# Products of a constant on the tensor engine in a planned encoder layer, with the plan's ties drawn from names

## The chip, the cores and the metric

The kernel runs on one core of a Trainium2 chip. A core has a tensor engine (PE, whose weight loads the profile lists apart as PEld), a vector engine (DVE), a scalar engine (ACT), a general engine (POOL) and a queue engine that issues transfers (SP). Each takes its own instructions in the order in which they were written, and waits for the others by semaphores. The metric is the device time of one execution in microseconds, the median of the runs.

## The reference, cut to what matters

One encoder layer on 512 tokens of width 1024 in float32: a layer norm, a mixer that joins neighbourhood attention with a bidirectional state-space branch (SSD), a layer norm, a squared-ReLU MLP, a layer norm.

```python
def reference(x, ...):
    h = layer_norm(x, ln0_g, ln0_b)
    mix = hybrid_mixer(h, w_in, conv_w, ..., w_attn_br, w_ssd_br, b_gate, w_o)
    h = layer_norm(DN_ALPHA * h + mix, ln1_g, ln1_b)
    return layer_norm(DN_ALPHA * h + sq_relu_mlp(h, w_ff1, w_ff2), ln2_g, ln2_b)

def hybrid_mixer(u, ...):
    q, k, v, z, xbc, dt_raw, gate = jnp.split(u @ w_in, offs, axis=-1)
    ya = neighbourhood_attention(q, k, v, rpb) @ w_attn_br
    xs, bm, cm = jnp.split(silu(centred_dwconv(xbc, conv_w, conv_b)), ...)
    y = ssd forward + ssd backward + xs * d_skip
    ys = group_rms_norm(y * silu(z)) * ssd_norm_w @ w_ssd_br
    return (sigmoid(gate0) * ya + sigmoid(gate1) * ys) @ w_o
```

The change touches nothing that is computed. It acts in the first layer norm, in the first projections, and on the order of the SSD branch.

## The kernel before, in words

Every product of two matrices is written as three (`mm3`, lines 352 to 354): both operands are split into a rounded part and a remainder, and high times high, high times low and low times high are summed in PSUM. So a weight slab `ws` that was loaded becomes `wh` (a copy on ACT, line 470) and `wl` (the difference, on DVE or POOL, line 473), and the normed tokens become `hTh` and `hTl`.

**The opening.** The 512 tokens come as four tiles `xt` of 128 tokens. DVE takes mean and variance of each (lines 507, 509), a few small steps on ACT and DVE give the scale (lines 515 to 526), and DVE writes the normed tile `xn` in two halves of 512 channels (line 532). PE transposes tiles 0 and 1 (half 0 of the tokens), later tiles 2 and 3 (half 1), 128 channels at a time, into four PSUM tiles `tp_h0_0_0` to `tp_h0_0_3` of two channel blocks each (line 561). Of each channel block k = 0 to 7, ACT makes `hTh` (line 568), ACT or DVE takes the bias off again (`hmb`, lines 574 and 578; in half 0 ACT for even k, DVE for odd k), and DVE makes `hTl` (line 585). The first projections `ps_x0_0` to `ps_x0_3` (B, C and two blocks of x of SSD group 0) take half 0 of the tokens first, k by k, three products a step: tiles `ps_x0_0` and `ps_x0_1` together are 48 products over 256 tokens and read the slab `bc0`. The first product of `ps_x0_2` reads the slab `x0`. The projection of dt (`ps_dt`) follows in between.

**The order.** From here to the end of the SSD branch nothing is written in the order of its engines. Each step is handed to `Plan.op` with its engine, a guess of its time, and the tiles that it reads and writes. `Plan.order` gives every step a rank (the longest chain of guesses behind it), and walks through a guess of the run: an engine that is free takes the ready step of the highest rank, on PE a "filler" (a projection) only when no chain step is ready. PSUM tiles and buffers are granted as counted by tags (`mm` 2, `tr` 2, `cb` 1, `yd` 1, `so` 2). The steps are then issued in the order of their guessed starts, and that is final. The ranks are first multiplied by small random factors, the `NUDGES`: each pair (seed, size) draws one factor per step. Before the change the draws go by the step's place in the list.

All later stages (attention, output projection, MLP) are ordered by the framework's own scheduler, outside the plan. `ones`, a 128x128 tile of 1.0 (memset on DVE, line 411), is used by one sum in the SSD branch (line 688).

Of the kernel before, what the change touches and what calls it, by code (L numbers as in the profile page):

```python
# [3 lines left out]

# [7 lines left out]
F32 = mybir.dt.float32  # L12
# [7 lines left out]
P = 128  # L20
# [20 lines left out]
BANKS = {"mm": 2, "tr": 2, "cb": 1, "yd": 1, "so": 2}  # L41
# [19 lines left out]

NUDGES = ((265225, 0.01), (410045, 0.001), (566648, 0.0005), (745606, 0.0005), (658272, 0.001), (17203, 0.0005),
          (943025, 0.0005), (429358, 0.001), (235890, 0.0005), (366213, 0.001))
XN_ENG = (("DVE", "DVE"),) * 4
LN0_BANKS = (("tr", "tr", "yd", "so"), ("tr", "tr", "yd", "tr"))
WDT = ("DVE", 0.66)
# [4 lines left out]
class Plan:  # L73
# [4 lines left out]
    TABLE = 1.28  # L78

    def __init__(self, tags):  # L80
        self.tags, self.ops, self.tiles = tags, [], {}

    class Tile:
        def __init__(self, plan, name, tag, make):
# [16 lines left out]

    def op(self, engine, us, fn, r=(), w=(), lock=False, table=None, filler=False, at=0.0):

        self.ops.append(dict(i=len(self.ops), e=engine, us=us, fn=fn, r=list(r), w=list(w), lock=lock,
                             table=table, filler=filler, at=at))

    def order(self, nudges=()):
        ops, n = self.ops, len(self.ops)
# [4 lines left out]
        for o in ops:  # L113
            i = o["i"]
# [21 lines left out]
        for t, u in users.items():  # L136
            tag = self.tiles[t].tag
# [11 lines left out]
        rank = [0.0] * n  # L149
        topo, deg = [], [len(p) for p in pred]  # L150
        stack = [i for i in range(n) if not deg[i]]
        while stack:
            i = stack.pop()
# [7 lines left out]
            rank[i] = ops[i]["us"] + max((rank[s] + (0 if ops[s]["e"] == ops[i]["e"] else self.LAT[ops[i]["e"]])  # L161
                                          for s in succ[i]), default=0.0)
        for seed, sigma in nudges:
            draw = random.Random(seed)
            rank = [r * (1.0 + sigma * draw.random()) for r in rank]
        free = dict(self.tags)
        left = {t: len(u) for t, u in users.items()}
        held = set()
# [14 lines left out]
        events, start, end = [0.0], [None] * n, [None] * n  # L183
# [3 lines left out]
        while done < n:  # L187
            while finish and finish[0][0] <= t:
                _, i = heapq.heappop(finish)
# [12 lines left out]
            for e in engines:  # L202
# [3 lines left out]
                for i in ready[e]:  # L206
                    o = ops[i]
# [10 lines left out]
                    key = (not o["filler"], rank[i]) if e == "PE" else (True, rank[i])  # L218
# [4 lines left out]
                i = best[1]  # L223
                o = ops[i]
# [5 lines left out]
                us = o["us"]  # L230
# [21 lines left out]
        return sorted(range(n), key=lambda i: (start[i], i))  # L252

    def replay(self, order, seed, spread):


        ops, n = self.ops, len(self.ops)
        at = {i: p for p, i in enumerate(order)}
        pred = [set(p) for p in self.pred]
        slots = {g: [None] * c for g, c in self.tags.items()}  # L260
# [12 lines left out]
        for i in reversed(order):  # L273
            queue.setdefault(ops[i]["e"], []).append(i)
# [32 lines left out]
    def issue(self):  # L307
        for i in self.order(NUDGES):
            self.ops[i]["fn"]()
# [3 lines left out]
def encoder_layer(ctx, tc, x, w_in, w_attn_br, w_ssd_br, w_o, w_ff1, w_ff2, pcols, rows64,  # L313
                  d_skip, ln_rows, rpb_pad, consts, lmask, out, dbg=None):
    nc = tc.nc
# [8 lines left out]
    psx = ctx.enter_context(tc.tile_pool(name="psx", bufs=1, space=PSUM))  # L324
# [85 lines left out]
    ones = gcp.tile([P, P], F32, name="ones")  # L410
    nc.vector.memset(ones, 1.0)
    eps = cp.tile([P, 1], F32, name="eps")
    nc.vector.memset(eps, EPS)
    warm = cp.tile([P, 1], F32, name="warm")
    nc.scalar.activation(warm, eps, AF.Sqrt)

# [29 lines left out]
    op = plan.op  # L446

    def bank(name, tag, shape):
        return plan.tile(name, tag, psx, shape, F32)
# [4 lines left out]
    def slab(name, parts, nk, ncol, engs):  # L454

        ws = plan.tile(f"ws_{name}", "ws", wp, [P, nk, ncol], F32)
        wh = plan.tile(f"wh_{name}", "wh", wp, [P, nk, ncol], F32R)
        wl = plan.tile(f"wl_{name}", "wl", wp, [P, nk, ncol], F32R)
        c = 0
        keys = []  # L460
        for j, (src, r0, c0, n) in enumerate(parts):
            op("SP", 4.0 * n / ncol, lambda src=src, r0=r0, c0=c0, n=n, c=c: nc.sync.dma_start(
                ws()[:, :, c : c + n],
                src[r0 : r0 + nk * P, c0 : c0 + n].rearrange("(k p) c -> p k c", p=P)),
               r=[("behind", 0)], w=[(ws.name, j)], at=4.8 if name == "x0" else 4.4)
            keys.append((ws.name, j))
            c += n
        hk = nk // 2
        for i, (k, eng) in enumerate(zip((slice(0, hk), slice(hk, nk)), engs)):
            op("ACT", 1.06, lambda k=k: nc.scalar.activation(wh()[:, k], ws()[:, k], AF.Copy),  # L470
               r=keys, w=[(wh.name, i)])
            e, us = ("DVE", 1.24) if eng is nc.vector else ("POOL", 2.42)
            op(e, us, lambda k=k, eng=eng: eng.tensor_tensor(  # L473
                out=wl()[:, k], in0=ws()[:, k], in1=wh()[:, k].bitcast(F32), op=ALU.subtract),
               r=keys + [(wh.name, i)], w=[(wl.name, i)], lock=True)
        return wh, wl
# [7 lines left out]
    xns = [plan.tile(f"xn{t}", "gt", gep, [P, D], F32) for t in range(NT)]  # L484
    def load_x(t):
# [7 lines left out]
       r=[(xts[0].name, 0)], w=[(xts[2].name, 0), ("behind", 0)])  # L493
# [11 lines left out]
    for t in range(NT):  # L505
        for j in range(2):
            op("DVE", 0.68, lambda t=t, j=j: v_.bn_stats(sts[t][:, j, :], xts[t]()[:, halves2[j]]),
               r=[(xts[t].name, 0)], w=[("st", t, j)])
        op("DVE", 0.2, lambda t=t: v_.bn_aggr(mv[:, t, :], sts[t]), r=[("st", t, 0), ("st", t, 1)],
           w=[("mv", t)])  # L510
    for ts in ((0,), (1,), (2, 3)):
# [4 lines left out]
           r=[("mv", t) for t in ts], w=[("vh", ts[0])], table="sqrt")  # L516
        op("DVE", 0.16, lambda pr=pr, nv=nv: v_.tensor_scalar(
            out=nv, in0=mv[:, pr, 1], scalar1=EPS, scalar2=-0.5, op0=ALU.add, op1=ALU.mult),
           r=[("mv", t) for t in ts], w=[("nv", ts[0])])
# [9 lines left out]
    for t in range(NT):  # L529
        for j, c in enumerate(halves2):  # L530
            if XN_ENG[t][j] == "DVE":
# [3 lines left out]
                   r=[("rs", t), (xts[t].name, 0)], w=[(xns[t].name, j)], lock=True)  # L535
            else:
# [9 lines left out]
       w=[(wh_dt.name, 0)])  # L546
    op(*WDT, lambda: (v_ if WDT[0] == "DVE" else nc.gpsimd).tensor_tensor(out=wl_dt(), in0=ws_dt(), in1=wh_dt().bitcast(F32),
                                                  op=ALU.subtract),
       r=[(ws_dt.name, 0), (wh_dt.name, 0)], w=[(wl_dt.name, 0)], lock=True)
    dtps = bank("ps_dt", "cb", [P, S])  # L550
    nb0 = gcp.tile([P, KD], F32, name="nb0")
    op("DVE", 0.1, lambda: v_.tensor_scalar(out=nb0, in0=pc[:, PC_B0 : PC_B0 + KD], scalar1=-1.0,
                                            scalar2=None, op0=ALU.mult), r=[("pc", 0)], w=[("nb0", 0)])
    for half in range(2):
        sl = slice(half * 256, (half + 1) * 256)
        tps = [bank(f"tp_h0_{half}_{i}", b, [P, 2, 2, P]) for i, b in enumerate(LN0_BANKS[half])]
        for t in range(2):
            for i, tpx in enumerate(tps):
                def f_tp(t=t, i=i, tpx=tpx, xn=xns[2 * half + t]):
# [3 lines left out]
                   w=[(tpx.name, t)])  # L563
        for k in range(KD):
# [5 lines left out]
               r=[(tpx.name, 0), (tpx.name, 1), ("pc", 0)], w=[("hTh", k, half)])  # L570

            hb_ = plan.tile(f"hmb{half}_{k}", "t1", sbp, [P, 2, 256], F32)
            if HMB_ENG[half][k] == "ACT":
                op("ACT", 0.51, lambda k=k, sl=sl, hb_=hb_: a_.activation(
                    hb_()[:, 0], hTh[:, k, sl].bitcast(F32), AF.Identity, bias=nb0[:, k : k + 1]),
                   r=[("hTh", k, half), ("nb0", 0)], w=[(hb_.name, 0)])
# [4 lines left out]
            else:  # L581
# [6 lines left out]
               r=[(tpx.name, 0), (tpx.name, 1), (hb_.name, 0)], w=[("hTl", k, half)])  # L588
        for k in range(KD):
# [3 lines left out]
               w=[(dtps.name, half)])  # L593
# [96 lines left out]
    for d, (tri, tag) in enumerate(((tri_f, "yd"), (tri_b, "yd"))):  # L690
# [428 lines left out]
    for s in range(2):  # L1119
# [9 lines left out]
        for b in range(4):  # L1129
# [5 lines left out]
                                    op=ALU.subtract)  # L1135
# [19 lines left out]
    for pr in range(NH // 2):  # L1155
# [20 lines left out]
        for hh, hp in enumerate(halves):  # L1176
# [3 lines left out]
                                    op=ALU.subtract)  # L1180
        for hh in range(2):
# [24 lines left out]
            for m2 in range(2):  # L1206
                pss = psx.tile([P, 2, 256], F32, tag="so", bufs=BANKS["so"], name=f"pss{h}_{m2}")
                for j in range(2):
# [5 lines left out]
                                     stop=True)  # L1214
# [66 lines left out]
    for d2 in range(4):  # L1281
# [3 lines left out]
        for j in range(2):  # L1285
            d = 2 * d2 + j
# [25 lines left out]
    for d2 in range(4):  # L1312
# [3 lines left out]
        for j in range(2):  # L1316
            d = 2 * d2 + j
# [6 lines left out]
                                    op=ALU.subtract)  # L1324
# [84 lines left out]
    for fq in range(NQ):  # L1409
# [3 lines left out]
        for s in range(4):  # L1413
# [5 lines left out]
            for j in range(2):  # L1419
                f = 2 * s + j  # L1420
# [3 lines left out]
                else:  # L1424
                    ps = psx.tile([P, S], F32, tag="mm", bufs=BANKS["mm"], name=f"ps_f1_{fq}_{f}")
                    for k in range(KD):
# [7 lines left out]
                                              op=ALU.subtract)  # L1434
# [17 lines left out]
        if not last:  # L1452
            for s in range(2):
# [7 lines left out]
                for t in range(NT):  # L1461
# [16 lines left out]
    for t in range(NT):  # L1478
# [10 lines left out]
        r = rsqrt(ffp, mv[:, 1:2], 1, f"2_{t}")  # L1489
# [68 lines left out]
```

## Time and profile before

| what | value |
|---|---|
| median of 3 runs | 1220.36 us (1219.28 to 1220.38) |
| the profiled execution, its own time | 1219.99 us |
| its span, first to last instruction | 1217.9 us |
| PE busy | 1185.8 us, 97% |
| DVE, ACT, POOL busy | 725.7 us (60%), 563.2 us (46%), 491.6 us (40%) |
| mean granted clock of PE | 0.993 |
| first transpose | 9.66 us |
| first product of the first projection | 14.96 us |
| PE busy in 0 to 20 us, in 20 to 40 us | 6.66 us, 19.75 us |

How to read it: times are from the first instruction on. A row of the timeline is start, duration, engine, line, operation, output<-inputs, shape, count, and in brackets how long the engine had been idle and what ended that. A busy time adds up spans that overlap, and matmuls are pipelined: their starts say more than their durations. The granted clock is the share of full speed that PE was given in a window. The plan's part ends at about 510 us.

### The profile page before, as it was taken

What the parts mean: (1) busy time and instruction counts of PE and PEld (TensorE: products, weight loads), DVE (VectorE), ACT (ScalarE), POOL (GpSimd) and SP (SyncE); (2) the same over time, 40 slices, a digit from 0 to 9 for tenths busy, and PEclk for the clock granted to TensorE, in tenths of its full rate; (3) what the DMA queues carried; (4) which work ended last, traced back from release to release, by engine and by line L of the source; (5) the groups of instructions that cost most, each with busy time, mean ns of one, the idle gap of its engine ahead of it and who ended that gap; (6) DMA issues with size and microseconds to landing.
All of it is one profiled execution on the core that took longest, in us unless ns stands there. A gap on an engine that the chain in (4) does not pass through costs nothing.

```text
span 1217.9 us, 16716 instructions
## 1 busy us (share of the span) xinstructions
PE 1185.8 (97%) x6378; PEld 1017.4 (84%) x6378; DVE 725.7 (60%) x1361; ACT 563.2 (46%) x946; POOL 491.6 (40%) x540
## 2 busy tenths in 40 slices
PE   5999999999999999999999989999999999999996
PEld 5988898989888888788888878899988888888885
DVE  7748475665666665534889874456654433443556
ACT  4576573836456463324677873432241331331510
POOL 1158967777787776203766720024320000000000
PEclk8999999999999999999999999999999999999998
DMA  6144243333324332234332233263114233322401
GB/s 230 53 143 139 90 136 104 120 109 119 110 98 142 113 110 70 69 104 118 83 87 62 70 129 94 90 222 124 36 69 126 81 104 104 104 91 85 160 28 52
DMA packets 124449, 127.19 MB, mean 104 GB/s; under 512 B 22353, under 2 KB 104913, under 8 KB 124369
## 3 DMA queue, kind: packets, MB, share of 16 engines
q1 hardware_dynamic: 124368, 126.13, 33.4%
q8 instruction: 50, 0.82, 0.3%
q14 instruction: 31, 0.25, 0.1%
HBM read 123.88 MB, written 2.23 MB: 104 GB/s over the span
## 4 chain that ended last, share of the span: by engine, by line
PE 88%; DVE 5%; ACT 3%; issue 2%; POOL 1%; DMA 1%; SPq 0%; DVEq 0%; POOLq 0%; ACTq 0%
PE ps_f L354 9%; PE ps_f L352 9%; PE ps_f L353 9%; PE ps_x L352 5%; PE ps_x L354 5%; PE ps_x L353 5%; PE ps_z L352 3%; PE ps_z L353 3%; PE ps_z L354 2%; PE yd L931 2%; PE ps_sbr L352 2%; PE ps_sbr L354 2%; PE ps_sbr L353 2%; PE ps_g L352 2%; PE ps_g L353 2%
## 5 line engine op out<-in xcount | busy, mean ns | idle before, releaser
L341 ACT ACTIVATE wh_f<-ws_f 128x1024 fp32r<-128x1024 f32 x60 | 60.1, 1052 | 118.6 <-PE ps_f L353 96.4
L740 DVE SCALAR_TENSOR_TENSOR cv<-ps_x,pc,cv 128x511 f32<-128x511 f32 (+1 forms) x128 | 95.7, 748 | 25.8 <-ACT cv L732 22.1
L353 PE MATMUL ps_f<-h1Th,wl_f 128*128 128x512 f32 (+1 forms) x288 | 104.6, 366 | 0.0
L352 PE MATMUL ps_f<-h1Th,wh_f 128*128 128x512 f32 (+1 forms) x288 | 104.4, 366 | 0.0
L354 PE MATMUL ps_f<-h1Tl,wh_f 128*128 128x512 f32 (+1 forms) x288 | 103.1, 367 | 1.0 <-DVE h1Tl L428 1.0
L342 DVE TENSOR_TENSOR wl_f<-ws_f,wh_f 128x1024 fp32r<-128x1024 f32 x60 | 72.7, 1251 | 45.3 <-ACT wh_f L341 45.1
L353 PE MATMUL ps_f<-wh_f,gl 128*128 128x512 f32 x224 | 86.8, 389 | 0.0
L354 PE MATMUL ps_f<-wl_f,gh 128*128 128x512 f32 x224 | 86.5, 389 | 0.0
L352 PE MATMUL ps_f<-wh_f,gh 128*128 128x512 f32 x224 | 86.3, 389 | 0.0
L352 PE MATMUL ps_z<-wh_z,hTh 128*128 128x256 f32 x256 | 75.9, 296 | 0.0
L354 PE MATMUL ps_z<-wl_z,hTh 128*128 128x256 f32 x256 | 72.4, 283 | 0.0
L353 PE MATMUL ps_z<-wh_z,hTl 128*128 128x256 f32 x256 | 72.4, 283 | 0.0
L1431 DVE TENSOR_TENSOR rl<-rl,ps_f 128x512 f32<-128x512 f32 x32 | 21.7, 687 | 69.1 <-ACT rl L1430 68.9
L1047 DVE TENSOR_TENSOR ysacc<-ps_sbr,ysacc 128x512 f32<-128x512 f32 x56 | 38.4, 688 | 40.4 <-PE ps_sbr L354 39.9
L354 PEld LDWEIGHTS ps_f<-h1Tl,wh_f 128*128 128x128 f32 x288 | 53.3, 188 | 9.9 <-DVE h1Tl L428 1.2
L352 PEld LDWEIGHTS ps_f<-h1Th,wh_f 128*128 128x128 f32 x288 | 54.1, 188 | 8.9
L353 PEld LDWEIGHTS ps_f<-h1Th,wl_f 128*128 128x128 f32 x288 | 54.2, 188 | 8.6
L1430 ACT ACTIVATE rl<-ps_f 128x512 f32<-128x512 f32 x32 | 19.0, 597 | 89.1 <-PE ps_f L354 85.6
L352 PE MATMUL ps_x<-hTh,wh_bc 128*128 128x512 f32 (+1 forms) x144 | 57.1, 396 | 1.6 <-ACT wh_bc L470 1.6
L352 PE MATMUL ps_sbr<-yTh,wh_sbr 128*128 128x512 f32 x128 | 55.8, 436 | 1.1 <-DVE ysacc L1047 0.5
L353 PE MATMUL ps_x<-hTh,wl_bc 128*128 128x512 f32 (+1 forms) x144 | 54.1, 376 | 2.0 <-POOL wl_bc L473 2.0
L1319 POOL TENSOR_TENSOR gt<-gt,ysacc 128x512 f32<-128x512 f32 x8 | 12.8, 1599 | 106.3 <-ACT gt L1059 98.1
(301 smaller groups left out, 3677.3 us busy)
## 6 DMA issues: line engine op xcount, KB each, us to landing
ws_f<-in_w_ff SPq DMA_DIRECT2D x32, 1024.0 KB
bc<-acs_d SPq DMA_DIRECT2D x32, 512.0 KB
ws_bc<-in_w_in SPq DMA_DIRECT2D x16, 512.0 KB
ws_x<-in_w_in SPq DMA_DIRECT2D x8, 1024.0 KB
ws_z<-in_w_in SPq DMA_DIRECT2D x8, 1024.0 KB
ws_g<-in_w_in SPq DMA_DIRECT2D x8, 1024.0 KB
ws_sbr<-in_w_ssd_br SPq DMA_DIRECT2D x8, 1024.0 KB
ws_qk<-in_w_in SPq DMA_DIRECT2D x16, 512.0 KB
```

The costliest lines, as they stand in the source:

```text
L341: nc.scalar.activation(hi[:, k], st[:, k], AF.Copy)
L342: (eng[i] if isinstance(eng, tuple) else eng).tensor_tensor(out=lo[:, k], in0=st[:, k], in1=hi[:, k].bitcast(F32), op=ALU.subtract)
L352: nc.tensor.matmul(o, lh, rh, start=start, stop=False)
L353: nc.tensor.matmul(o, ll, rh, start=False, stop=False)
L354: nc.tensor.matmul(o, lh, rl, start=False, stop=stop)
L740: op("DVE", 0.75, lambda j=j, o=o, n=n: nc.vector.scalar_tensor_tensor(out=acc()[:, o], in0=ps()[:, n], scalar=tap(j), in1=acc()[:, o], op ...
L931: nc.tensor.matmul(yd()[:, c % 2, h * HD : (h + 1) * HD], bc()[:, 1, h, :], xtok()[:, c, h * HD : (h + 1) * HD], start=True, stop=True)
L1047: op("DVE", 0.69, lambda d=d, ps=ps: nc.vector.tensor_tensor(out=ysacc[:, d, :], in0=ps(), in1=ysacc[:, d, :], op=ALU.add), r=[(ps.name, 0 ...
L1319: nc.gpsimd.tensor_tensor(out=g1, in0=g1, in1=ysacc[:, d, :], op=ALU.mult)
L1430: nc.scalar.activation(rl, ps, AF.Relu)
L1431: nc.vector.tensor_tensor(out=rl, in0=rl, in1=ps, op=ALU.mult)
```

## The change

1. Right after `ones` is set, and ahead of the plan, 44 products of `ones` with itself are put on PE (`WARM`), into a PSUM tile of the tag `yd` that nobody reads.
2. Inside the plan, 12 more of them (`WARM2`) are steps on PE with a guess of 0.22 us each. They read the second half of tile 1's `xn` (`xns[1]`, 1), so they can't start ahead of it, write a PSUM tile of the tag `cb`, and nobody reads that either.
3. The draws of the nudges no longer go by place but by name: a step's key is the name of the tile that it writes and a running number, and the factor is a checksum of the seed and that key. The ten pairs are replaced by six others. So the whole order of the plan is a new one.

```diff
+WARM = 44
+WARM2 = 12
...
+        k = w[0][0], self.named.setdefault(w[0][0], 0)
+        self.named[w[0][0]] += 1
...
         for seed, sigma in nudges:
-            draw = random.Random(seed)
-            rank = [r * (1.0 + sigma * draw.random()) for r in rank]
+            rank = [r * (1.0 + sigma * zlib.crc32(b"%d " % seed + o["key"]) / 2.0 ** 32)
+                    for r, o in zip(rank, ops)]
...
+    idle = psx.tile([P, 2, P], F32, tag="yd", bufs=BANKS["yd"], name="idle")
+    for i in range(WARM):
+        nc.tensor.matmul(idle[:, i % 2, :], ones, ones, start=True, stop=True)
...
+    idle2 = bank("idle2", "cb", [P, 2, P])
+    for i in range(WARM2):
+        op("PE", 0.22, lambda i=i: nc.tensor.matmul(idle2()[:, i % 2, :], ones, ones, start=True,
+                                                    stop=True), r=[(xns[1].name, 1)],
+           w=[(idle2.name, 0)])
```

**First place: PE, from its first instruction.** In the names, `tp_h_0_2` is half 0 and the third PSUM tile; `xn_151` and `xn_161` are tiles 0 and 1 before the change, `xn_191` and `xn_204` the same two after it. Before:

```order
L561 MATMUL tp_h_0_0_154<-cst,xn_151 128x128 x2
L561 MATMUL tp_h_0_1_158<-cst,xn_151 128x128 x2
L561 MATMUL tp_h_0_2_163<-cst,xn_151 128x128 x2
L561 MATMUL tp_h_0_3_166<-cst,xn_151 128x128 x2
L561 MATMUL tp_h_0_2_163<-cst,xn_161 128x128 x2
L561 MATMUL tp_h_0_3_166<-cst,xn_161 128x128 x2
L561 MATMUL tp_h_0_0_154<-cst,xn_161 128x128 x2
L561 MATMUL tp_h_0_1_158<-cst,xn_161 128x128 x2
L352 MATMUL ps_x_0_203<-hTh,wh_bc_172 128x256
```

After the change, in the same place:

```order
L422 MATMUL idle<-ones 128x128 x44
L575 MATMUL tp_h_0_1_198<-cst,xn_191 128x128 x2
L575 MATMUL tp_h_0_0_201<-cst,xn_191 128x128 x2
L575 MATMUL tp_h_0_1_198<-cst,xn_204 128x128 x2
L575 MATMUL tp_h_0_0_201<-cst,xn_204 128x128 x2
L575 MATMUL tp_h_0_3_213<-cst,xn_204 128x128 x2
L575 MATMUL tp_h_0_2_216<-cst,xn_204 128x128 x2
L561 MATMUL idle_222<-ones 128x128
L575 MATMUL tp_h_0_3_213<-cst,xn_191 128x128 x2
L575 MATMUL tp_h_0_2_216<-cst,xn_191 128x128 x2
L561 MATMUL idle_222<-ones 128x128 x11
L357 MATMUL ps_x_0_250<-hTh,wh_bc_219 128x256
```

The 44 products stand ahead of every transpose, and the 12 around and behind the last ones, ahead of the first projection. The first PSUM tile that has both tokens' tiles is finished by the sixth transpose; before it was the fourteenth.

**Second place: ACT, from the first scale factors on.** `hTh<-tp_h_0_3` is one channel block of half 0 that is read from the fourth PSUM tile, and `hmb_6` is the block k = 6. Before:

```order
L515 ACTIVATE ln_v<-ln_mv,eps 128x1 x2
L470 ACTIVATE wh_bc_172<-ws_bc_119 128x1024
L568 ACTIVATE hTh<-tp_h_0_0_154,pc 128x256 x2
L470 ACTIVATE wh_bc_172<-ws_bc_119 128x1024
L574 ACTIVATE hmb_0_189<-hTh,nb_96 128x256
...
L568 ACTIVATE hTh<-tp_h_0_2_163,pc 128x256
L574 ACTIVATE hmb_4_225<-hTh,nb_96 128x256
L470 ACTIVATE wh_x_232<-ws_x_125 128x1024 x2
L545 ACTIVATE wh_dt<-ws_dt 128x512
```

After:

```order
L524 ACTIVATE ln_v<-ln_mv,eps 128x1 x2
L582 ACTIVATE hTh<-tp_h_0_1_198,pc 128x256
L479 ACTIVATE wh_bc_219<-ws_bc_164 128x1024
L582 ACTIVATE hTh<-tp_h_0_0_201,pc 128x256
L588 ACTIVATE hmb_0_236<-hTh,nb_141 128x256
...
L582 ACTIVATE hTh<-tp_h_0_3_213,pc 128x256
L479 ACTIVATE wh_x_282<-ws_x_170 128x1024 x2
L588 ACTIVATE hmb_6_301<-hTh,nb_141 128x256
L554 ACTIVATE wh_dt<-ws_dt 128x512
```

Before, half of the slab `wh_bc` was split ahead of the first `hTh`; now the first `hTh` leads. Before, the last `hmb` of half 0 stood ahead of the two halves of `wh_x`; now it stands behind them. Between the first `hTh` and the last `hmb` stand eight `hTh`, four `hmb` and, before, one half of a slab; now four halves.

**Third place: DVE, at the last `hTl` of half 0.** The last three of the eight channel blocks and what follows, before:

```order
L585 SCALAR_TENSOR_TENSOR hTl<-tp_h_0_2_163,pc,hmb_5_217 128x256
L578 TENSOR_SCALAR hmb_7_230<-hTh,pc 128x256
L585 SCALAR_TENSOR_TENSOR hTl<-tp_h_0_3_166,pc,hmb_7_230 128x256
L585 SCALAR_TENSOR_TENSOR hTl<-tp_h_0_2_163,pc,hmb_4_225 128x256
L507 BN_STATS ln_st_91<-xt_113 128x6
```

After:

```order
L599 SCALAR_TENSOR_TENSOR hTl<-tp_h_0_2_216,pc,hmb_4_275 128x256
L599 SCALAR_TENSOR_TENSOR hTl<-tp_h_0_3_213,pc,hmb_7_284 128x256
L516 BN_STATS ln_st_137<-xt_168 128x6
L518 BN_AGGR ln_mv<-ln_st_136 128x2
L518 BN_AGGR ln_mv<-ln_st_137 128x2
L599 SCALAR_TENSOR_TENSOR hTl<-tp_h_0_3_213,pc,hmb_6_301 128x256
L526 TENSOR_SCALAR ln_v<-ln_mv 128x2
L531 RECIPROCAL ln_rs<-ln_v 128x2
```

The last block was k = 4; now it is k = 6, and the scale of tiles 2 and 3 (from line 526 on) follows straight behind it.

Outside the plan every engine's order is what it was. On SP the identity for the transposes is issued one place earlier, ahead of `pc`, the columns of gains and biases.

More of the change, by code (lines that the diff above doesn't have):

```diff
@@ L2 @@
 import random
+import zlib
 from contextlib import ExitStack
@@ L60 @@
 CC_N = 896
-NUDGES = ((265225, 0.01), (410045, 0.001), (566648, 0.0005), (745606, 0.0005), (658272, 0.001), (17203, 0.0005),
-          (943025, 0.0005), (429358, 0.001), (235890, 0.0005), (366213, 0.001))
+NUDGES = ((301112, 0.002), (606439, 0.0005), (237741, 0.0005), (121095, 0.0005), (300588, 0.01),
+          (143396, 0.0005))
+WARM = 44
+WARM2 = 12
 XN_ENG = (("DVE", "DVE"),) * 4
@@ L80, in __init__ @@
     def __init__(self, tags):
-        self.tags, self.ops, self.tiles = tags, [], {}
+        self.tags, self.ops, self.tiles, self.named = tags, [], {}, {}
     class Tile:
@@ L102, in op @@
     def op(self, engine, us, fn, r=(), w=(), lock=False, table=None, filler=False, at=0.0):
-        self.ops.append(dict(i=len(self.ops), e=engine, us=us, fn=fn, r=list(r), w=list(w), lock=lock,
+        k = w[0][0], self.named.setdefault(w[0][0], 0)
+        self.named[w[0][0]] += 1
+        self.ops.append(dict(i=len(self.ops), key=f"{k}".encode(), e=engine, us=us, fn=fn, r=list(r), w=list(w), lock=lock,
                              table=table, filler=filler, at=at))
```

## Prediction

> **What bounds the kernel now.** I read the page first, then the list of PE's waits, then the timeline of the first 30 us, then windows cut to the steps of the granted clock.
>
> ```profile
> PE 1185.8 (97%) x6378; PEld 1017.4 (84%) x6378; DVE 725.7 (60%) x1361; ACT 563.2 (46%) x946; POOL 491.6 (40%) x540
> ...
> PE tp_h L561 <- DVE xn L532: 9.7, 1, 9.7
> PE ps_x L353 <- POOL wl_bc L473: 2.0, 1, 2.0
> ...
> PE ps_x L352 <- ACT wh_bc L470: 1.6, 1, 1.6
> ```
>
> PE is the bound: 32 us of the span is all it is not busy, and 13.3 us of that is the three waits of the opening. The same list for 24 to 503 us alone, the rest of the planned part, has three rows and 1.5 us:
>
> ```profile
> PE yd L931 <- issue: 0.6, 1, 0.6
> PE ps_sbr L352 <- DVE ysacc L1047: 0.5, 1, 0.5
> PE ps_sbr L352 <- ACT yTh L1024: 0.4, 1, 0.4
> ```
>
> So a better order of the plan can return 1.5 us there and no more. The rest has to come from the opening. Its timeline:
>
> ```profile
> 0.83 0.17 DVE L411 MEMSET ones<- 128x128 f32 x1 [0.83 <-PEq L1549]
> 9.06 0.54 DVE L532 TENSOR_SCALAR xn<-xt,ln_mv,ln_rs 128x512 f32<-128x512 f32 x1
> 9.59 1.45 DVE L532 TENSOR_SCALAR xn<-xt,ln_mv,ln_rs 128x512 f32<-128x512 f32 x3
> 9.66 3.67 PE L561 MATMUL tp_h<-cst,xn 128*128 128x128 f32 x16 [9.66 <-DVE xn L532]
> 9.99 1.06 ACT L470 ACTIVATE wh_bc<-ws_bc 128x1024 fp32r<-128x1024 f32 x1 [2.40 <-DMA ws_bc<-in_w_in]
> 12.94 1.02 ACT L568 ACTIVATE hTh<-tp_h,pc 128x256 fp32r<-128x256 f32 x2 [1.90 <-PE tp_h L561]
> 14.96 0.38 PE L352 MATMUL ps_x<-hTh,wh_bc 128*128 128x256 f32 x1 [1.63 <-ACT wh_bc L470]
> 14.98 2.35 POOL L473 TENSOR_TENSOR wl_bc<-ws_bc,wh_bc 128x1024 fp32r<-128x1024 f32 x1 [10.51 <-ACT wh_bc L470]
> 17.39 0.58 PE L353 MATMUL ps_x<-hTh,wl_bc 128*128 128x256 f32 x1 [2.05 <-POOL wl_bc L473]
> 19.16 0.51 ACT L574 ACTIVATE hmb<-hTh,nb 128x256 f32<-128x256 f32 x1
> 19.57 1.99 ACT L470 ACTIVATE wh_x<-ws_x 128x1024 fp32r<-128x1024 f32 x2
> 20.05 0.88 DVE L585 SCALAR_TENSOR_TENSOR hTl<-tp_h,pc,hmb 128x256 fp32r<-128x256 f32 x2
> 20.98 0.58 PE L354 MATMUL ps_x<-hTl,wh_bc 128*128 128x256 f32 x1 [0.21 <-DVE hTl L585]
> ```
>
> From 12.94 on ACT is hardly idle until the last `hmb` ends at 19.67, and the last `hTl` of half 0, at 20.93, lets PE go at 20.98. Between 9.66 and 20.98 it is not PE that sets the pace, it is the ACT chain that starts with the first finished transposes. From 20.98 PE is saturated. What an edit is worth here is read there: when PE is let go for good, how many products it still owes, and at which clock it does them.
>
> The clock, in windows cut at its changes, and three more windows late in the run:
>
> ```profile
> 13.30:16.95 3.65, 0.41 (x2) 0.19 (x1) 3.06 (x7) 3.62 (x8) 1.97 (x1) 1.00 1.07 347
> 16.95:20.37 3.42, 2.98 (x13) 2.82 (x13) 3.10 (x8) 3.33 (x7) 0.39 (x1) 0.50 0.55 156
> 20.37:23.78 3.41, 3.20 (x15) 2.91 (x15) 3.20 (x10) 1.89 (x4) 2.38 (x1) 0.50 0.10 30
> 23.78:27.20 3.42, 3.42 (x31) 3.42 (x31) 3.42 (x7) 0.00 (x0) 0.00 (x0) 1.00 0.17 27
> 713.27:716.68 3.41, 2.07 (x14) 1.65 (x14) 2.32 (x8) 2.28 (x4) 1.28 (x1) 1.00 0.00 0
> 716.68:720.10 3.42, 1.97 (x12) 1.71 (x13) 1.60 (x7) 1.72 (x4) 0.00 (x0) 1.00 0.21 78
> 720.10:723.51 3.41, 3.41 (x10) 2.62 (x9) 3.41 (x6) 3.41 (x8) 0.00 (x0) 0.50 0.91 336
> ```
>
> The clock stands at 0.50 from 16.95 to 23.78, twice 3.41 us. It is decided every 3.41 us by what PE did in the interval before: busy 0.41 of 3.65 drops it, 1.97 of 3.42 drops it, 2.07 of 3.41 doesn't; 2.98 of 3.42 doesn't lift it, 3.20 of 3.41 does. The 1.00 of the first window is no measurement of the transposes: sixteen took 3.67 us, 0.23 each, and at full clock six take 0.66 (next rows), 0.11 each. They ran at half; they filled the interval to 13.54 and lifted the clock, so that the product at 14.96 took 0.38 where the one at 17.39 took 0.58. [...]
>
> Of the chain that ended last, one projection product at half clock, one at full, and six transposes at full:
>
> ```profile
> 21.56 0.21 PE ps_x L352
> ...
> 25.10 0.12 PE ps_x L352
> ...
> 27.91 0.66 PE tp_h L561 x6
> ```
>
> and of the timeline of PE, a product in full float32 (`pcs`) and its follower:
>
> ```profile
> 65.15 0.39 PE L687 MATMUL pcs<-dts,cst 128*128 128x128 f32 x2
> 65.37 0.60 PE L688 MATMUL pcs<-dts,ones 128*128 128x256 f32 x2
> ```
>
> **The change part by part.** *The 44 products.* A float32 product of this size is two records: the two at 65.15 make way 0.22 us later. So 44 are 88 records, 0.11 each at full clock, and 0.23 at half, by the transposes. They start when `ones` is set, 1.05. If the grid lies as in this run (16.95, back by 3.41: 6.71, 3.30), the interval to 3.30 is filled by two thirds only, and the clock rises at 6.71. Until then 5.66 / 0.23 = 25 records are done; the other 63 take 7.0: the burst ends at 13.7. Earliest rise: nine tenths of an interval filled, 4.1, end 12.3. Latest: two intervals, 7.9, end 14.3. In every case that is behind 11.04, where DVE has all of tiles 0 and 1 ready: the burst costs PE 2.6 to 4.6 us of transposing against 9.66, and the transposes get 0.11 for 0.23.
>
> *The ACT chain's start.* The first bank with both tiles is now done by the sixth transpose instead of the fourteenth (12.65 at 0.23 each; ACT followed 0.3 later). 13.7 + 5 x 0.11 + 0.3 = 14.55 against 12.94: 1.6 late (ends: 0.2, 2.2). [...]
>
> *The ACT chain's length.* Before, 12.94 to 19.67: 6.73 for eight `hTh`, four `hmb` and one slab half. Now one more half of `wh_bc` (1.06, which before lay under the transposes at 9.99) and both halves of `wh_x` (1.99) stand ahead of the last `hmb`: 9.78. From 14.55 that is 24.33, and with 0.1 and 0.5 for `hTl` 24.95: PE is let go 3.95 later than at 20.98.
>
> *What PE still owes then.* Before, one product at 14.96 and thirteen in the window from 16.95 were done, 34 of 48 were left, and thirteen of them ran at 0.21. Now the wait falls at the seventh step's last product: 28 are left, all at 0.12, 3.4 us, so 28.3. Before, the same place, the first product of the next tile, was 26.38:
>
> ```profile
> 21.46 0.61 ACT L545 ACTIVATE wh_dt<-ws_dt 128x512 fp32r<-128x512 f32 x1
> 21.98 0.28 ACT L515 ACTIVATE ln_v<-ln_mv,eps 128x2 f32<-128x2 f32 x1
> 23.01 0.15 DVE L522 RECIPROCAL ln_rs<-ln_v 128x2 f32<-128x2 f32 x1
> ...
> 25.00 1.91 DVE L532 TENSOR_SCALAR xn<-xt,ln_mv,ln_rs 128x512 f32<-128x512 f32 x4
> ...
> 26.38 0.28 PE L352 MATMUL ps_x<-hTh,wh_x 128*128 128x256 f32 x1
> ```
>
> 1.9 us late: the clock pays half of the delay back. *Tiles 2 and 3:* their scale stands behind the last `hTl` on DVE, and their square root behind `wh_dt` (0.6) on ACT. 24.33 + 0.6 + 0.3 lets the reciprocal go at 25.25; before, 3.9 us lay from it (23.01) to the last `xn` (26.91), so 29.15, 2.2 late. PE, 1.9 late, waits 0.2 for that. The opening costs 2.1 us (with the ends of the burst: 0.7 to 2.7).
>
> *The 12 products* take 2.6 us up to 18.1 (13.7, sixteen transposes 1.8, twelve 2.6). Their cover is POOL: its 2.35 us of `wl_bc` start when the first half of `wh_bc` ends (14.55 + 0.5 + 1.06 = 16.1) and end at 18.45, and PE's second projection product waits for that. Nothing; with POOL out of the way they would hold PE for up to 1.4 us.
>
> *The new order behind 30 us:* 1.5 us of waits could go, as many could come: 0, between -1.5 and +1.5. *The drop at 720* costs half of 3.41, 1.7 us, and hung on 1.97 against 2.07 of busy time, so on where the grid falls: 0, or -1.7. The moved identity load on SP is needed long after; nothing.
>
> Sum on the profiled execution: 1219.99 + 2.1 = 1222.1. The median of the runs is 0.4 above that execution: 1222.5. About 0.2% (2.4 us: 1217.9 to 1222.8) is what a measurement here can tell from no change.
>
> **The rivals.** *A, the forecast:* the burst overruns, the chain is late, the clock holds. 0.42; by its terms 1220.9 to 1224.0.
>
> *B, slower: the clock falls behind the burst.* From 18.1 to 24.95 PE has 20 products for 6.9 us, each step two close together and one alone, 0.12 + 0.28 + 0.28 of busy time: 0.68 x 7 = 4.8, 69%. The point from which it decides lies between 1.97 of 3.42 (58%) and 2.07 of 3.41 (61%). An uneven spread is enough to drop one interval; then PE owes its 28 products and twelve transposes at half clock for one to two intervals behind 24.95: 1.7 to 2.9 us on top. 1224.2 to 1225.4, say 1225. For it: the margin is 0.3 us. 0.25.
>
> *C, nothing comes out:* an early rise (burst end 12.3, opening +0.7) and an order that sheds its waits: 1220. 0.17.
>
> *D, faster:* PE has full clock all along the burst, 9.7 us, end 10.75. Then the chain starts at 11.6, PE is let go at 22.0 and reaches the next tile at 25.4 against 26.38, -1.0; with the drop at 720 gone -2.7, with the waits gone -4.2: about 1217. Against it: the 0.23 of the first transposes, which began after 9.66 us of rest as the burst does after one. Only all terms together pass the bound. 0.12.
>
> *E, the change doesn't do what it says:* products of ones don't lift the clock. 88 x 0.23 = 20.2, burst end 21.3, everything eight us late, some of it repaid: 1228. The interval to 13.54 was filled by transposes, products with an identity, and lifted it. 0.04.
>
> **How the numbers follow.** Slower: 0.16 of A (its upper part, above 1222.8), 0.24 of B, E: 0.44. Faster: 0.11 of D, 0.02 of C: 0.13. The rest: 0.43. Range 1218.0 to 1226.0: it leaves out most of D, E, and the top of B. A's own range is 1220.9 to 1224.0.
>
> **What would show it.** Right: 88 more PE records from 1.05 on, at 0.2 and then 0.1 us; first transpose between 12 and 14.5; first `hTh` about 0.9 behind it; PE let go by `hTl` about 25 with 28 products left; clock 1.00 there. Wrong: a first transpose ahead of 11 (D), a clock row of 0.50 between 20 and 31 (B), records at 0.23 to the burst's end (E), or waits of PE of over 2 us between 30 and 500, of which the trace of before has none.

## The result and the profile after

The changed kernel takes 1230.3 us in the median of seven runs (1225.21 to 1231.31), the kernel before 1221.32 (1219.28 to 1222.93, seven runs): 1.0065 times as long, 95% interval 1.0046 to 1.0084. Slower, and by 9 us where 2.1 were forecast (1222.5 against the 1220.36 known then). Two of the seven runs took 1225.2 and five 1229.5 to 1231.3. The profiled one is of the quick two: 1225.21 us, of which the span is 1223.4.

Where the time came in is seen at three places that PE passes in both kernels: the first `ps_z` product (the end of the opening), the first `ps_v` product (the end of the planned part), and the first `ps_o` product (behind the stretch in which the clock dropped at 720). The timeline of PE before:

```profile
52.22 0.28 PE L352 MATMUL ps_z<-wh_z,hTh 128*128 128x256 f32 x1
...
511.27 0.47 PE L352 MATMUL ps_v<-wh_v,hBh 128*128 128x512 f32 x1 [1.21 <-ACT wh_v L341]
...
808.44 0.28 PE L352 MATMUL ps_o<-wh_o,mgh 128*128 128x256 f32 x1
```

and after:

```profile
53.91 0.28 PE L357 MATMUL ps_z<-wh_z,hTh 128*128 128x256 f32 x1
...
518.05 0.47 PE L357 MATMUL ps_v<-wh_v,hBh 128*128 128x512 f32 x1 [1.21 <-DVE hBh L1131]
...
813.91 0.28 PE L357 MATMUL ps_o<-wh_o,mgh 128*128 128x256 f32 x1
```

The opening is 1.7 us longer. From `ps_z` to `ps_v` it was 459.0 and is 464.1: **5.1 us more in the planned part**, where the forecast had 0. From `ps_v` to `ps_o` it was 297.2 and is 295.9, 1.3 less. That is the whole of the 5.5 us between the two at `ps_o`.

The opening ran as forecast in its mechanism, but for the clock. The timeline after:

```profile
1.05 11.89 PE L422 MATMUL idle<-ones 128*128 128x128 f32 x88 [1.05 <-DVE eps L418]
12.78 1.47 PE L575 MATMUL tp_h<-cst,xn 128*128 128x128 f32 x12
13.64 0.56 ACT L582 ACTIVATE hTh<-tp_h,pc 128x256 fp32r<-128x256 f32 x1 [4.96 <-PE tp_h L575]
14.75 2.62 PE L561 MATMUL idle<-ones 128*128 128x128 f32 x22
15.22 2.37 POOL L482 TENSOR_TENSOR wl_bc<-ws_bc,wh_bc 128x1024 fp32r<-128x1024 f32 x1 [10.68 <-ACT wh_bc L479]
17.64 0.38 PE L358 MATMUL ps_x<-hTh,wl_bc 128*128 128x256 f32 x1 [0.16 <-POOL wl_bc L482]
24.14 0.58 PE L359 MATMUL ps_x<-hTl,wh_bc 128*128 128x256 f32 x1
```

The burst ends at 12.9, the first `hTh` is at 13.64, PE is let go at 24.14, and the 12 products lie under POOL's `wl_bc`. The clock, in windows cut at its grid, the first two in the opening and the other two around 725:

```profile
18.51:21.92 3.41, 1.23 (x8) 1.03 (x8) 3.13 (x8) 3.25 (x7) 0.01 (x1) 1.00 0.41 105
21.92:25.33 3.41, 3.40 (x14) 2.87 (x14) 3.27 (x14) 2.07 (x4) 2.42 (x1) 0.50 0.18 54
...
721.65:725.06 3.41, 2.07 (x16) 1.69 (x15) 1.85 (x7) 1.19 (x2) 0.47 (x1) 1.00 0.00 0
725.06:728.47 3.41, 2.03 (x9) 1.38 (x9) 2.58 (x8) 3.21 (x7) 0.00 (x0) 1.00 0.68 162
```

It fell for one interval behind the burst, and in this run it did not fall near 725. The list of PE's waits from 24 to 510 us, which before had three rows and 1.5 us, has now:

```profile
PE ps_z L357 <- DVE cv L754: 1.8, 1, 1.8
PE yo L959 <- DVE t L971: 1.3, 1, 1.3
PE yo L959 <- DVE hst L916: 0.8, 1, 0.8
PE ps_sbr L357 <- ACT sz L799: 0.7, 1, 0.7
PE tp_b L826 <- ACT cv L757: 0.7, 1, 0.7
```

That is 5.3 us against 1.5, or 3.8 more. Of the 5.1 it leaves 1.3 in pieces that this list doesn't hold. The two largest were followed to their start. In the timeline of POOL, DVE and PE (start, duration, engine; two instructions on the rows with x2):

```profile
220.74 5.24 POOL L482 TENSOR_TENSOR wl_z<-ws_z,wh_z 128x1024 fp32r<-128x1024 f32 x2 [1.81 <-ACT wh_z L479]
220.89 5.68 DVE L935 COPY_PREDICATED bc<-msk,bc 128x512 f32<-128x512 int32 x2
...
237.46 0.35 PE L357 MATMUL ps_z<-wh_z,hTh 128*128 128x256 f32 x1 [1.78 <-DVE cv L754]
...
250.60 5.18 POOL L482 TENSOR_TENSOR wl_bc<-ws_bc,wh_bc 128x1024 fp32r<-128x1024 f32 x2 [0.52 <-ACT wh_bc L479]
250.62 2.95 DVE L935 COPY_PREDICATED bc<-msk,bc 128x512 f32<-128x512 int32 x1
...
254.20 0.70 PE L959 MATMUL yo<-hst,cv 128*128 128x256 f32 x2 [1.33 <-DVE t L971]
```

and that line's own group (least, median and most ns of one copy):

```profile
L935 DVE COPY_PREDICATED bc<-msk,bc x32: 718/759/2952, 85.6 to 459.9; 128x512 f32<-128x512 int32 x32
```

DVE's copy under a mask (`COPY_PREDICATED`) took 2.95 us where it began 0.02 us behind POOL's subtraction, and two took 5.68 where the first began 0.15 behind; the median is 0.76. Each copy that is caught so loses some 2.2 us. Behind 220.89 that is 4.3 us, and PE waits ahead of 237.46 for DVE's `cv`, which comes late by it; behind 250.62 it is 2.2 us, and PE waits ahead of 254.20 for `t`, which stood behind the copy. The trace of before had such meetings too, at places where PE waited for nothing, so no list of waits showed them (a pair of copies that was caught at 338.22 in the new order cost PE no wait either):

```profile
258.92 5.23 POOL L473 TENSOR_TENSOR wl_x<-ws_x,wh_x 128x1024 fp32r<-128x1024 f32 x2
259.00 2.92 DVE L921 COPY_PREDICATED bc<-msk,bc 128x512 f32<-128x512 int32 x1
```

The times fit a copy that stands until POOL's first half is done: half of a pair of POOL's without a meeting (4.75 for the pair, in experiment 5) and a copy of 0.7 would make 3.1 for the copy that comes second, and it took 2.95. That is an estimate from these times; what holds the copy back no run shows. POOL loses too, 5.2 for the pair. Whether the copy lost went with which of the two began first, in one copy of the same order. In the trace of after it began 0.06 us ahead of POOL and took 0.76, and it was POOL's half that lost, 2.91 for 2.4; in that of experiment 2 it began 0.03 behind and took 2.98. After:

```profile
206.71 0.76 DVE L935 COPY_PREDICATED bc<-msk,bc 128x512 f32<-128x512 int32 x1
206.77 2.91 POOL L482 TENSOR_TENSOR wl_x<-ws_x,wh_x 128x1024 fp32r<-128x1024 f32 x1 [0.61 <-ACT wh_x L479]
```

and in experiment 2:

```profile
205.72 5.23 POOL L478 TENSOR_TENSOR wl_x<-ws_x,wh_x 128x1024 fp32r<-128x1024 f32 x2 [0.62 <-ACT wh_x L475]
205.75 2.98 DVE L931 COPY_PREDICATED bc<-msk,bc 128x512 f32<-128x512 int32 x1
```

The planner keeps these two kinds of instruction apart in its own times (both carry its `lock`). By its code the new list has the second of the two copies end at 219.30 and the subtraction for `wl_z` start at 219.30, and the copy that ran at 250.62 and its `wl_bc` meet at 246.93 in the same way. The margin is nothing, and nothing in the program holds the second engine back: on the chip POOL was first.

### The profile page after: what moved, and what is told of

It is laid out like the page before. It is cut to its first block, busy times and chain, and to the rows that moved or that the text cites. A ratio compares the mean times of both kernels' runs of the same rounds, so it can differ in the third digit from the quotient of the medians.

```text
span 1223.4 us, 16931 instructions
## 1 busy us (share of the span) xinstructions
PE 1197.1 (98%) x6490; PEld 1027.0 (84%) x6490; DVE 732.0 (60%) x1361; ACT 557.5 (46%) x941; POOL 486.8 (40%) x540
## 4 chain that ended last, share of the span: by engine, by line
PE 82%; DVE 10%; ACT 3%; issue 2%; DMA 1%; SPq 0%; POOL 0%; DVEq 0%; ACTq 0%; POOLq 0%
PE ps_f L359 9%; PE ps_f L357 9%; PE ps_f L358 9%; PE ps_x L359 4%; PE ps_x L357 4%; PE ps_x L358 4%; PE ps_z L357 2%; PE ps_z L358 2%; PE ps_z L359 2%; PE ps_sbr L357 2%; PE ps_sbr L359 2%; PE ps_sbr L358 2%; PE yd L945 2%; PE yo L959 2%; PE ps_g L357 2%
## 5 line engine op out<-in xcount | busy, mean ns | idle before, releaser
L931 DVE TENSOR_TENSOR bc<-bc,amd 128x512 f32<-128x512 f32 x32 | 33.9, 1060 | 37.4 <-DMA bc<-acs_d 37.4
L359 PE MATMUL ps_x<-hTl,wh_bc 128*128 128x512 f32 (+1 forms) x144 | 53.9, 374 | 2.3 <-DVE hTl L599 2.3
L357 PE MATMUL ps_x<-hTh,wh_bc 128*128 128x512 f32 (+1 forms) x144 | 54.5, 378 | 0.1
```

What stands on the lines that cost most here:

```text
L357: nc.tensor.matmul(o, lh, rh, start=start, stop=False)
L359: nc.tensor.matmul(o, lh, rl, start=False, stop=stop)
L931: op(e, us, lambda d=d, eng=eng, c=c, bc=bc: eng.tensor_tensor(out=bc()[:, d], in0=bc()[:, d], in1=by_dir(amd, c, g)[:, d, :].unsqueeze(2) ...
```

## The experiments

Before them stood **theory O**: the new order of the planned part costs the 5 us, by its own waits, and the burst costs the opening alone. Its rival was **T**, that the burst upsets the plan by starting it later. For the mechanism inside O there were two: **C**, the collisions of DVE's copies with POOL, and **R**, that PE has too few products in front whatever DVE does. A table of all kernels first. The ratio is to runs of the kernel before on the same chip: their medians are 1220.83 for 1 to 4, 1221.73 for 5 to 8 and 1221.63 for 9 and 10. The four last columns are of the profiled run, by the same three places of PE's timeline and the first `ps_abr` product.

| kernel | median us (runs) | ratio to before, 95% | profiled us | first `ps_z` | to `ps_v` | `ps_abr` to `ps_o` |
|---|---|---|---|---|---|---|
| before | 1221.32 (7) | 1 | 1219.99 | 52.22 | 459.05 | 88.79 |
| after | 1230.3 (7) | 1.0046 to 1.0084 | 1225.21 | 53.91 | 464.14 | 87.38 |
| 1 old order, 44 | 1222.49 (11) | 1.0007 to 1.0026 | 1224.12 | 53.60 | 460.68 | 89.72 |
| 2 new order, no burst | 1225.89 (5) | 1.0032 to 1.0060 | 1226.98 | 52.34 | 464.78 | 89.93 |
| 3 old order, 22 | 1219.79 (11) | 0.9987 to 1.0004 | 1221.27 | 51.05 | 460.06 | 90.03 |
| 4 new order, 22 | 1227.01 (5) | 1.0043 to 1.0068 | 1227.01 | 51.63 | 465.90 | 88.79 |
| 5 after, two waits | 1224.77 (6) | 1.0016 to 1.0040 | 1224.57 | 54.81 | 462.43 | 87.37 |
| 6 old order, filled | 1218.0 (9) | 0.9962 to 0.9984 | 1216.48 | 50.01 | 459.04 | 87.37 |
| 7 after, again | 1229.01 (4) | 1.0055 to 1.0094 | 1228.58 | 54.02 | 465.81 | 88.79 |
| 8 no nudges | 1240.84 (4) | 1.0144 to 1.0172 | 1241.10 | 53.42 | 478.15 | 88.71 |
| 9 new order, two waits, no burst | 1222.94 (12) | 0.9996 to 1.0023 | 1222.15 | 51.67 | 460.80 | 89.78 |
| 10 after, mended | 1220.57 (11) | 0.9986 to 1.0003 | 1219.86 | 51.51 | 460.94 | 87.38 |

The last column shows the clock from the first `ps_abr` product on (719.65 before): 87.4 without a half-clock interval, 88.7 to 88.8 with one, 89.7 to 90.0 with two. In 4 and 8 one more such interval lay ahead of that product, which the column doesn't hold.

**1. The old order with the burst.** The kernel before, with this ahead of its `warm`:

```diff
+    idle = psx.tile([P, 2, P], F32, tag="yd", bufs=BANKS["yd"], name="idle")
+    for i in range(44):
+        nc.tensor.matmul(idle[:, i % 2, :], ones, ones, start=True, stop=True)
```

> The old order of the plan with the burst of 44 products ahead of it and without the 12. If the new order costs the 5 us that the traces show between 30 and 510 us (theory O), this kernel pays the opening alone: 1.7 us, less 1.4 if the clock's drop at 720 us goes, so 0 to 2 us above the kernel before, 1221.3 to 1223.3. If the waits in the plan come from the burst, which sets the engines against the transfers later than the planner took it (theory T), it is 4 to 9 us slower, 1225 to 1230.

1222.49, as O has it: the opening is 1.4 longer, and T falls as the cause of the five us. In the profiled run, at 1224.12 one of the longer ones, the planned part is 1.6 longer than in the profile of before with the same order; the largest piece is a wait that neither before nor experiments 3 and 6 have:

```profile
PE yo L949 <- DVE t L961: 1.3, 1, 1.3
```

So one order, with another start, can differ by as much as I had allowed for a change of the order.

**2. The new order without the burst.**

```diff
-    idle = psx.tile([P, 2, P], F32, tag="yd", bufs=BANKS["yd"], name="idle")
-    for i in range(WARM):
-        nc.tensor.matmul(idle[:, i % 2, :], ones, ones, start=True, stop=True)
```

> The new order with its 12 products, without the burst of 44. Theory O: 3.5 to 7 us slower than the kernel before, 1225 to 1228, with waits of PE of 4 to 6 us between 30 and 510 us, at L353-type products behind DVE's cv and at yo behind DVE's t and hst. Theory T: 1219 to 1222.5, with under 2 us of such waits.

1225.89; the opening is before's to 0.1 us, and the planned part is 5.7 longer, with after's own waits:

```profile
PE ps_z L356 <- DVE cv L750: 1.8, 1, 1.8
PE yo L955 <- DVE t L967: 1.3, 1, 1.3
PE yo L955 <- DVE hst L912: 0.9, 1, 0.9
```

O holds: the order makes its waits with or without the burst. The 12 products stayed in every kernel of the new order, so the new draws and those 12 steps are not told apart.

**3 and 4. Half the burst**, with the old order (against 1) and with the new (against after):

```diff
-    for i in range(44):
+    for i in range(22):
...
-WARM = 44
+WARM = 22
```

> The old order with half the burst, 22 products. They end at 8 to 9 us, ahead of the first scaled tile at 9.66, so the transposes start no later and run at 0.11 each. Under either theory the chain on ACT starts up to 1 us earlier than before (12 to 12.9) and the time is 1219.0 to 1222.0; if over 1223, the burst costs by something other than its length.

> The changed kernel with 22 products for 44. The opening is 1.5 to 2.5 us earlier than with 44. Theory O: the waits of the plan stay, 1223 to 1228 by whichever of the two groups of times it falls in. Theory T: half the delay, so most of the waits go, 1219 to 1223.

In the timeline of 3 the burst of 22 is over before a tile is ready, and the transposes run at full clock from their usual start:

```profile
9.89 2.12 PE L565 MATMUL tp_h<-cst,xn 128*128 128x128 f32 x16 [1.55 <-DVE xn L536]
...
11.83 1.02 ACT L572 ACTIVATE hTh<-tp_h,pc 128x256 fp32r<-128x256 f32 x2 [0.30 <-PE tp_h L565]
```

`hTh` starts 1.1 earlier than before, a little more than expected, and `ps_z` 1.2; 1219.79 lies inside what was expected and can't be told from before. With the new order the opening is 2.3 us shorter than with 44, as expected, and the planned part is no shorter. Its profile also shows what a wait of that order can set off (windows):

```profile
231.80:235.20 3.40, 1.63 (x14) 1.46 (x14) 3.29 (x6) 2.08 (x4) 2.36 (x2) 1.00 0.00 0
235.20:238.61 3.41, 3.41 (x17) 3.41 (x18) 0.34 (x1) 2.23 (x3) 2.34 (x2) 0.50 0.00 0
```

The wait of 1.8 us left PE 1.63 busy of 3.40, and the clock fell for the interval behind it; the planned part is 1.8 longer than after's. In the profiles of after and of 2, where the grid lay otherwise, the interval with most of the same wait had PE busy for 2.13 (from 233.55) and 1.94 of 3.41 (from 233.07), and the clock held.

**5. The two collisions taken away.** The changed kernel, the order on every engine as it was, with one wait more on each of two of POOL's subtractions:

```diff
+BEHIND = {("z3", 0): "bc3_2", ("bc4", 1): "bc4_3"}
...
+                if (name, i) in BEHIND:
+                    tc.add_manual_dep(sub.ins, done[BEHIND[name, i]].ins.name, mybir.DependencyInfo(
+                        mybir.DependencyClass.Sync, mybir.DependencyReason.DATA), reason="behind the mask")
```

> The changed kernel, same order on every engine, with two waits added on POOL: the subtraction for wl_z of group 3 starts behind DVE's copy under a mask for bc of that group (the third), and the one for wl_bc of group 4 behind the copy for the fourth bc. Theory C (the copies are caught behind POOL's 2.4 us subtractions, 2.2 us lost on DVE each time, and that makes PE's waits at 235 and 252 us): the three copies take 0.7 to 1.3 us again, the two waits (1.9 and 1.5 us) go, the profiled run is 3 to 3.5 us shorter than the same kind of run of the changed kernel, median 1225 to 1228. Rival R (PE has too few products in front there, whatever DVE does): the waits stay over 1 us each, median 1229 to 1231.

1224.77, 4.2 below the changed kernel on the same chip (experiment 7). The timeline of DVE and POOL:

```profile
222.21 1.38 DVE L944 COPY_PREDICATED bc<-msk,bc 128x512 f32<-128x512 int32 x2
223.81 4.74 POOL L486 TENSOR_TENSOR wl_z<-ws_z,wh_z 128x1024 fp32r<-128x1024 f32 x2 [3.62 <-DVE bc L944]
...
249.94 0.73 DVE L944 COPY_PREDICATED bc<-msk,bc 128x512 f32<-128x512 int32 x1
250.91 4.75 POOL L486 TENSOR_TENSOR wl_bc<-ws_bc,wh_bc 128x1024 fp32r<-128x1024 f32 x2 [1.51 <-DVE bc L944]
```

and the waits of PE from 24 to 510 us:

```profile
PE tp_b L835 <- ACT cv L766: 1.9, 3, 0.9
PE yo L969 <- DVE hst L925: 1.0, 1, 1.0
PE ps_sbr L358 <- ACT sz L808: 0.7, 1, 0.7
```

The three copies take 1.38 (two) and 0.73 in place of 5.68 and 2.95, POOL's pairs 0.4 to 0.5 less each, and both waits are gone. The planned part, 462.4, is to be held against 7's 465.8, which has the same three waits at `tp_b`: 3.4 less. C holds, R falls. (The first `ps_z` is late, at 54.81: in this run the clock stood at half for two intervals from 21.07, in that of after for one.) That the median fell by more than 3.4 fits with runs in which the wait at 235 dropped the clock as in 4; that was not seen in a profile of the changed kernel.

**6. The old order, with PE's waits filled.** Experiment 3, and eight products ahead of the first projection product, nine behind it, and six in each of PE's last two waits ahead of 720:

```diff
+            fill(8)
             nc.tensor.matmul(ps()[:, sl], a, hTh[:, k, sl], start=k == 0, stop=False)
+            fill(9)
+            gaps.clear()
...
+            if h == NH - 1:
+                rest("a", 6, last.ins)
...
+    rest("b", 6, last.ins)
```

> The old order with 22 products at the start, 8 ahead of the first projection product, 9 behind it, and 6 each in PE's two last waits ahead of 720 us. If the clock is held by them: no row of 0.50 between 7 and 30 us, the 48th projection product at 23.2 to 24.2 against 25.1 with the 22 alone, no row of 0.50 at 720; median 1216 to 1218.5. If they only delay PE: the 48th at 25 or later, 1219 to 1222.

1218.0, 0.9973 of before (0.9962 to 0.9984). The clock stays at 1.00 from 4.69 to 1209.6. Its windows in the opening and ahead of 720:

```profile
14.93:18.34 3.41, 2.74 (x22) 2.34 (x21) 3.16 (x8) 3.33 (x8) 1.26 (x1) 1.00 0.90 293
18.34:21.76 3.42, 2.54 (x22) 2.33 (x21) 3.28 (x8) 2.77 (x5) 2.22 (x1) 1.00 0.36 103
...
716.40:719.80 3.40, 3.40 (x19) 2.61 (x18) 2.97 (x9) 3.38 (x7) 0.00 (x0) 1.00 0.49 189
```

and the 48th projection product in its timeline, at 26.25 before:

```profile
23.89 0.28 PE L743 MATMUL ps_x<-hTl,wh_bc 128*128 128x256 f32 x1
```

So fillers pay here when they are over before the tile that the next product waits for: 2.2 us in the opening, of which the 22 at the start alone had 1.2 (3), and 1.4 at 720.

**7. The changed kernel again**, for a profile of its slower group.

> The changed kernel once more, for a profile of a run of about 1230. Theory M (the five us between its two groups of times are intervals at half clock, behind the wait at 235 us and at 727, 1.7 us each, and one more in the opening): such a run shows three half-clock intervals more than the run of 1225 and waits of the same length. Rival W: the waits between 30 and 510 us themselves are longer by 3 to 5 us in such a run, and the clock rows agree.

Neither theory alone. The profiled run of 1228.58 is 3.4 longer than that of 1225.21. 1.4 of it is one interval at half clock behind 728.62, where PE had been busy 1.90 of 3.42:

```profile
725.20:728.62 3.42, 1.90 (x12) 1.62 (x13) 1.61 (x7) 1.64 (x3) 0.00 (x0) 1.00 0.21 77
728.62:732.04 3.42, 3.42 (x10) 2.65 (x9) 3.42 (x6) 3.42 (x8) 0.00 (x0) 0.50 0.97 320
```

1.7 is the planned part, of which 1.3 is a wait that came once in the other run and here three times:

```profile
PE tp_b L826 <- ACT cv L757: 2.0, 3, 0.9
```

The runs of 1229.4 to 1232.6 were not caught in a profile; what they have on top stays open, and so does why `tp_b` waits more often in some runs.

**8. No nudges at all**, both bursts kept:

```diff
-NUDGES = ((301112, 0.002), (606439, 0.0005), (237741, 0.0005), (121095, 0.0005), (300588, 0.01),
-          (143396, 0.0005))
+NUDGES = ()
```

> The changed kernel with an empty list of nudges: the planner's plain order, with both bursts. It shows how far an order of this planner can lie from another: theory O has it anywhere from 1222 to 1232 with its own waits between 30 and 510 us, 2 to 10 us in sum; if it lies at 1222 to 1224 with under 2 us of waits, the changed list is a bad draw; if over 1230, the old list was a good one.

1240.84, outside what I expected, above. By the reading set down there, the old list was a good one. Its planned part is 19 us longer than before's, with 14.2 us of waits of PE from 24 to 525 us and two intervals at half clock from 129.61; the rest was not followed. The three largest waits:

```profile
PE tp_b L825 <- ACT cv L756: 3.5, 4, 1.0
PE yo L958 <- DVE t L970: 3.2, 2, 1.6
PE ps_z L356 <- ACT sz L798: 2.4, 1, 2.4
```

**9 and 10. Do the terms add up?** 9 is the new order with the edits of 2 and 5; 10 is the changed kernel with the edits of 4 and 5 and the twelve products of 6 ahead of 727:

```diff
+BEHIND = {("z3", 0): "bc3_2", ("bc4", 1): "bc4_3"}
...
-WARM = 44
+WARM = 22
...
+            if h == NH - 1:
+                rest("a", 6, last.ins)
...
+    rest("b", 6, last.ins)
```

> The new order with its 12 products and the two waits on POOL, without the burst of 44. Theory C has the two collisions as 3.3 us of the order's 5: with them gone and the opening as before, 1222 to 1223.5, still 1 to 2 us above the kernel before by the waits that are left (hst at 83, sz at 132, tp_b at 277 us). If the order's cost is spread over many small losses instead, 1224 to 1226.

> The changed kernel with 22 products for 44, the two waits on POOL, and 6 products each in PE's two last waits ahead of 727 us. If opening, collisions and the clock's drop add up: 0.6 less than before for the opening, 2 more for the waits that are left, up to 2.8 less for the drops at 727: 1219.5 to 1222.5. If over 1223, a term is missing.

1222.94 and 1220.57, both inside. The planned part of both is 1.8 to 1.9 longer than before's: that is the new order without its two collisions, with `hst` (0.8 to 1.0), `sz` (0.7) and `tp_b` (0.8) still waited for. The old order's own profiles reach from 459.0 to 460.7, so this rest is hardly more than its spread. The last column of 10 is 87.38, no drop. Mended so, the changed kernel can't be told from the kernel before, and it doesn't reach experiment 6. In the kernels with other numbers of products (1 to 4, 6, 9, 10) a few neighbouring steps of PE and DVE between 727 and 743 us swap places; the change itself swaps two such pairs on DVE there.

## Why the prediction was wrong

- **The burst:** its end, 13.7 (12.3 to 14.3), was 12.9: right, and earlier because the clock rose at 4.86 and not 6.71 (18 of the burst's records in the 3.81 us up to there, 32 in the next 3.41). The grid lay elsewhere than in the run before, which was the stated condition.
- **The chain:** first `hTh` 0.86 behind the first transpose against 0.85, PE let go at 24.14 against 24.95, with 28 products left as forecast. The opening cost 1.7 against 2.1 (0.7 to 2.7). Mechanism and size right, but for the clock (next point); experiment 1 gives 1.4 for the burst with the old order. One reading of the order was off: before, the tenth transpose was the first to finish a PSUM tile; the fourteenth finished `tp_h_0_0`, which ACT takes first, so the sum stands.
- **The clock behind the burst (rival B):** it did fall, for one interval, so "the clock holds" of A failed, and B's sign, a row of 0.50 between 20 and 31, came. In that interval PE was busy 1.23 of 3.41 us, not 69%, because the products came in lumps: PE waited 1.16 us ahead of 19.55 and 1.14 ahead of 21.70. The price was not B's 1.7 to 2.9: of the half-clock interval only 1.2 us lay behind 24.14, which by estimate cost half of that, 0.6. In the total of 1.7 that loss is contained, since the burst had ended 0.8 earlier than forecast. That the profiled run came out at B's 1225 is chance: the planned part made it.
- **The 12 products** cost nothing, under POOL's `wl_bc`, as argued: PE's next wait for POOL was 0.16.
- **The transposes** ran at 0.12 each (twelve in 1.47), against the 0.11 of the forecast and 0.23 before (sixteen in 3.67).
- **The drop at 720:** 0 or -1.7; it was -1.4 in the profiled run and 0 in that of 7. PE was busy there for 2.03 of 3.41 us in the profiled run (from 725.06) and for 1.90 of 3.42 in 7 (from 725.20): it went with where the grid lay, as said. But no point between 58% and 61% of busy time shows in all the profiles: the clock held with 1.67 of 3.41 in 8, 49%, and fell with 2.04 in 1, 60% (last section).
- **The step that failed** is "1.5 us of waits could go, as many could come: 0, between -1.5 and +1.5". It measured +5.1 (profiled run), +5.7 (2), +6.8 (7). The bound was taken from the old order's waits, by symmetry. The waits that one order has left say nothing on those that another brings; the empty list of experiment 8 brings 19. Of the 5.1 to 5.7, the two places where DVE is caught behind POOL make 3.4 (5 against 7) to 4.0 (9 against 2), and the rest 1.8 to 1.9 (3.4 in 5 and 7, with two more waits at `tp_b`). The price of a collision, 2.2 us of DVE, stood in the trace of before at 259.00. I had read which waits PE has, not how long DVE's copies take beside POOL.
- **The sign** that I named for this, a wait of over 2 us between 30 and 500, didn't come: the longest is 1.78. Five of 0.7 to 1.8 did the same.
- **The median** lies 5.1 us above the profiled run, where the forecast had 0.4. So of the 7.8 us by which it missed, 3.1 are in the profiled run (5.1 more in the planned part, less 1.4 at 720 and 0.4 in the opening, within 0.2) and 4.7 in how runs of one kernel differ. Of the 3.4 by which 7's profiled run is longer, 1.4 is a half-clock interval and 1.3 the waits at `tp_b`; why most runs of the changed kernel are that long stays open. Experiment 2, the same order without the burst, has no such gap (1225.89 against 1226.98 profiled). By the medians, each against its own runs of before, the burst costs 2.2 us (7) to 3.9 (the first seven runs) with the new order, more than the 1.7 of the opening. So O's second half, that it costs the opening alone, is not shown.

## What to carry to other kernels

A new list of nudges to a list scheduler is a new kernel: its waits are bounded by other orders of the same planner, not by the waits of the old one, and where it sets instructions of two engines end to end with no margin, look whether the trace has that pair's price when they meet (here 2.2 us of DVE for one copy). Products that keep the clock up must be over when the work they wait for is ready; here half a burst and fillers in the right waits were together worth 3.6 us in the profiled run, and a burst that overran cost 1.4. Where a wait of one engine starts at a slow instruction of another, follow the slow one to its neighbour in time before blaming the order.

## What the runs showed of the hardware

- A copy under a mask on DVE took 0.76 us where it began 0.06 us ahead of POOL's subtraction (after) and 2.98 where the same copy began 0.03 behind (2); POOL's pair of subtractions took 5.23 in 2, and in 5, where two other pairs met no copy, 4.74 and 4.75.
- The clock's grid lay elsewhere in each of the first six profiles of the table: its first rise came at 13.54, 4.86, 4.62, 14.61, 5.49 and 6.51 us. The later changes that the windows show lie whole steps of 3.413 us from there: in before 16.95 is 1 step on, and 723.51 is 208.
- The busy time of PE in an interval of the grid went with the clock of the next one only roughly. It held with 2.03 (after, from 725.06), 1.94 (2, from 233.07) and 1.67 of 3.41 us (8, from 242.25); it fell with 1.97 (before, from 716.68) and with 2.04 (1, from 718.00).
